# Thirty-two bytes of padding per partition on the split operands of a float32r transformer kernel

## The chip, the cores and the metric

The kernel runs on one core of one Trainium2 chip. The metric is the device time of one execution in microseconds, shown as the median over runs. In the tables below PE is TensorE (matmuls), PEld the loading of its stationary operand, DVE is VectorE, ACT ScalarE, POOL GpSimd and SP SyncE.

## The reference

A sequence of 512 tokens with 1024 features passes through two blocks. The first is a feed-forward layer (SwiGLU), a mixer (dilated-window attention plus a pooled branch, both gated), and a second SwiGLU. The second block has two layers, each a mixer (top-k sparse attention in layer 0, a state-space scan in layer 1) followed by a convolutional feed-forward:

```python
def swiglu(x, w1, w3, w2):
    return (jax.nn.silu(x @ w1) * (x @ w3)) @ w2
...
def conv_ffn(h, w_up, conv_w, conv_b, w_down):
    up = h @ w_up
    up = lax.conv_general_dilated(
        up, conv_w[:, None, :], window_strides=(1,), padding=[(CONV_W - 1, 0)],
        dimension_numbers=('NWC', 'WIO', 'NWC'), feature_group_count=2 * D_FF) + conv_b
    val, gate = jnp.split(up, 2, axis=-1)
    return (jax.nn.silu(gate) * val) @ w_down
```

D_MODEL is 1024, D_FF is 2816, and everything is float32.

## The kernel before

**Three matmuls for one product.** Activations lie feature-major: eight tiles of 128 features by 512 tokens. Each float32 factor is split into a high part h (rounded to float32r by an ACT copy) and a low part l (the rest, by a subtraction), and a product is made of three float32r matmuls (`mm3`, L260 to L262): weight-high times activation-high, weight-high times activation-low, weight-low times activation-high. In `gemm` the stationary operand is 128 columns of a weight tile, and the moving operand is a whole activation tile of 512 columns. In `token_gemm` it is the other way round: 128 tokens of an activation tile are stationary, the weight tile moves. Some of its calls take every fourth token (`by4`), so that the stationary operand is read with a stride of four elements.

**Weights.** `weight` (L238 to L247) issues one DMA of 512 KB into a `raw` tile on SP's queue, copies it to `wh` on ACT (L245) and subtracts it into `wl`, nearly always on DVE (L246). There are four `raw` buffers and three each of `wh` and `wl`.

**Activations.** `xt()` gives tiles of pool `xp` (24 buffers, name `x`). They hold the residual stream and the split inputs of every feed-forward, of the mixer and of the gated unit after the scan. In the feed-forwards the gated product is split into `u` tiles (pool `up`, 16 buffers, opened anew for each feed-forward), which are the moving operands of the second product. The mixer keeps its later split operands in tiles `mu` and `m`, the sparse attention in `du`; the change doesn't touch those.

**Order.** The program runs in this order: SwiGLU 1, mixer, SwiGLU 2, sparse attention, convolutional feed-forward 0, scan and gated unit, convolutional feed-forward 1. The order of instructions on each engine is that of the code; `pump()` slips pieces of background work (modulation vectors, top-k selection, state-space preparation) between weight tiles.

**Where the tiles lie.** Pools are laid one after another in each partition's memory, and the buffers of a pool follow each other without a gap. An `x`, `u` or `t` buffer has 2048 bytes, a `raw`, `wh` or `wl` buffer 4096, all multiples of 512. So all buffers of a pool have one offset modulo 512, and a pool that follows a pool of such buffers has the same one. In the program as built these offsets are:

| tiles | offset modulo 512 bytes |
|---|---|
| raw, wh, wl, x, t | 224 |
| u in both SwiGLUs and in convolutional feed-forward 1 | 224 |
| u in convolutional feed-forward 0 (behind the pool of the state-space preparation) | 96 |
| mu and m (mixer) | 0 |
| du (sparse attention) | 384 |

A 128-column slice of a weight tile starts at a multiple of 512 bytes in it, so the stationary operand of `gemm` is always at 224.

Of the kernel before, what the change touches and what calls it, by code (L numbers as in the profile page):

```python
# [12 lines left out]
F32R = mybir.dt.float32r  # L13
# [6 lines left out]
P = 128  # L20
T = 512
# [151 lines left out]
def emit(nc, tc, A, out):  # L173
    es = ExitStack()
    with es:
        cp = es.enter_context(tc.tile_pool(name="cp", bufs=1))
        raw = es.enter_context(tc.tile_pool(name="raw", bufs=4))
        wp = es.enter_context(tc.tile_pool(name="wp", bufs=3))
        xp = es.enter_context(tc.tile_pool(name="xp", bufs=24))
# [6 lines left out]
        def nm(s):  # L186
            uid[0] += 1
            return f"{s}{uid[0]}"

        def xt(dt=F32):  # L190
            return xp.tile([P, T], dt, name=nm("x"), tag="x")

        def tt(w=T, dt=F32):
            return tp.tile([P, w], dt, name=nm("t"), tag="t")
# [13 lines left out]
        def col(name, k):  # L208
            return vec[:, VEC[name][0] + k : VEC[name][0] + k + 1]
# [13 lines left out]
        def pump():  # L223
            rate[1] += rate[0]
            while rate[1] >= 1.0:
                rate[1] -= 1.0
                while bg:
                    try:
                        next(bg[0])
                        break  # L230
                    except StopIteration:
                        bg.pop(0)
# [6 lines left out]
        def weight(ap, w=1024, eng=V):  # L239
            pump()  # L240
            r = raw.tile([P, 1024], F32, name=nm("raw"), tag="raw")
            nc.sync.dma_start(r[:, :w], ap)
            h = wp.tile([P, 1024], F32R, name=nm("wh"), tag="wh")
            l = wp.tile([P, 1024], F32R, name=nm("wl"), tag="wl")
            S.activation(h[:, :w], r[:, :w], AF.Copy)  # L245
            eng.tensor_tensor(l[:, :w], r[:, :w], h[:, :w].bitcast(F32), op=ALU.subtract)  # L246
            return h, l  # L247

        X = []
        for k in range(KT):  # L250
            t = xt()
            nc.sync.dma_start(t, A["xT"][:, k])
            X.append(t)
            if k == 0:
                first = weight(A["f1u"][0])
# [8 lines left out]
        def gemm(w, XH, XL, o=0, ps=None):  # L264
            ps = psa() if ps is None else ps
            n = len(XH)
            for k in range(n):
                s = slice((o + k) * P, (o + k + 1) * P)
                mm3(ps, w[0][:, s], w[1][:, s], XH[k], XL[k], k == 0, k == n - 1)
            return ps  # L270
# [45 lines left out]
        def spread(y, o=0):  # L316
            p = psb()
            for b in range(4):
                E.matmul(
                    p[:, b * P : (b + 1) * P],  # L320
                    y[:, o + b : o + b + 1].to_broadcast([P, P]), ident, start=True, stop=True,
                )
            return p

        def kept(p):
            t = cp.tile([P, T], F32, name=nm("rb"), tag="rb")
            S.activation(t, p, AF.Copy)
            return t

        def norm(parts):  # L330
            p = psb()
            meansq(p, 0, parts)
            v = const([P, 4])
            V.tensor_scalar(v, p[:, :4], 1e-6, None, op0=ALU.add)
            for j in range(1, len(parts)):
                V.tensor_tensor(v, v, p[:, 8 * j : 8 * j + 4], op=ALU.add)
            y = const([P, 4])
            rsq(v, y, 4)
            return y

        def split_scaled(t, g):
            h, l = xt(F32R), xt(F32R)
            S.activation(h, t, AF.Copy, scale=g)  # L343
            V.scalar_tensor_tensor(l, t, g, h.bitcast(F32), op0=ALU.mult, op1=ALU.subtract)
            return h, l
# [37 lines left out]
        def swiglu_ffn(name, gname, up, acc, then, pre=()):  # L383
            pre = list(pre)
            XH, XL = [], []
            for k in range(KT):
                h, l = split_scaled(X[k], col(gname, k))
                XH.append(h)
                XL.append(l)
            Rb = None  # L390
            for f0, n in FGROUPS:
                UH, UL = [], []
                for f in range(f0, f0 + n):
                    p1 = gemm(pre.pop(0) if pre else weight(A[name + "u"][2 * f]), XH, XL)
                    if Rb is None:
                        Rb = kept(spread(norm(acc.parts())))
                    p3 = gemm(weight(A[name + "u"][2 * f + 1]), XH, XL)
                    a, b = tt(), tt()
                    V.tensor_tensor(a, p1, Rb, op=ALU.mult)
                    S.activation(a, a, AF.Silu)  # L400
                    V.tensor_tensor(b, p3, Rb, op=ALU.mult)  # L401
                    G.tensor_tensor(b, a, b, op=ALU.mult)  # L402
                    h = up.tile([P, T], F32R, name=nm("u"), tag="u")
                    l = up.tile([P, T], F32R, name=nm("u"), tag="u")
                    S.activation(h, b, AF.Copy)
                    G.tensor_tensor(l, b, h.bitcast(F32), op=ALU.subtract)
                    UH.append(h)
                    UL.append(l)
                for m in range(KT):
                    w = weight(A[name + "d"][m, :, f0 * P : (f0 + n) * P], n * P)  # L410
                    p = gemm(w, UH, UL)
                    V.scalar_tensor_tensor(X[m], p, 0.5, X[m], op0=ALU.mult, op1=ALU.add)
                    if f0 == FGROUPS[-1][0]:
                        for t in then:
                            t.add(m)
# [297 lines left out]
        def modulate(Rb, gs):  # L713
            g, sh = gs
            HH, HL, done = [], [], []
            for k in range(KT):
                t = tt()
                h, l = xt(F32R), xt(F32R)
                with tc.issue_after(done[k - 2].ins) if k > 1 else nullcontext():
                    V.scalar_tensor_tensor(t, X[k], g[:, k : k + 1], Rb, op0=ALU.mult, op1=ALU.mult)  # L720
                S.activation(h, t, AF.Identity, bias=sh[:, k : k + 1])
                done.append(
                    V.scalar_tensor_tensor(l, t, sh[:, k : k + 1], h.bitcast(F32), op0=ALU.add, op1=ALU.subtract)
                )
                HH.append(h)
                HL.append(l)
            return HH, HL, done[-1]
# [258 lines left out]
        def conv_ffn(i, up, acc, then=None):  # L986
            Rb = spread(norm(acc.parts()))
            HH, HL, _ = modulate(Rb, GS["f", i])

            def conv(p, j, t):  # L990
                S.activation(t, p, AF.Identity, scale=col(f"cw{i}", 88 + j), bias=col(f"cb{i}", j))
                V.scalar_tensor_tensor(t[:, 1:], p[:, : T - 1], col(f"cw{i}", 44 + j), t[:, 1:], op0=ALU.mult, op1=ALU.add)
                V.scalar_tensor_tensor(t[:, 2:], p[:, : T - 2], col(f"cw{i}", j), t[:, 2:], op0=ALU.mult, op1=ALU.add)

            for f0, n in FGROUPS:
                UH, UL = [], []
                for f in range(f0, f0 + n):
                    p1 = gemm(weight(A[f"u{i}"][2 * f]), HH, HL)
                    a, b = tt(), tt()
                    conv(p1, f, a)  # L1000
                    p3 = gemm(weight(A[f"u{i}"][2 * f + 1]), HH, HL)
                    conv(p3, f + NF, b)
                    S.activation(b, b, AF.Silu)  # L1003
                    G.tensor_tensor(b, a, b, op=ALU.mult)  # L1004
                    h = up.tile([P, T], F32R, name=nm("u"), tag="u")
                    l = up.tile([P, T], F32R, name=nm("u"), tag="u")
                    S.activation(h, b, AF.Copy)  # L1007
                    G.tensor_tensor(l, b, h.bitcast(F32), op=ALU.subtract)  # L1008
                    UH.append(h)
                    UL.append(l)  # L1010
                for m in range(KT):
                    w = weight(A[f"d{i}"][m, :, f0 * P : (f0 + n) * P], n * P)
                    p = gemm(w, UH, UL)
                    V.scalar_tensor_tensor(X[m], p, MOD[i][:, 40 + m : 41 + m], X[m], op0=ALU.mult, op1=ALU.add)  # L1014
                    if f0 == FGROUPS[-1][0]:
                        if then is None:
                            nc.sync.dma_start(out[:, m], X[m])
                        else:
                            then.add(m)
# [327 lines left out]
```

## Time and profile before

| what | value |
|---|---|
| median of 3 runs | 2470.77 us (2466.86 to 2472.44) |
| span of the profiled execution | 2468.1 us |
| PE busy | 2341.6 us, 95% of the span |
| DVE busy | 1479.9 us, 60% |
| ACT busy | 886.5 us, 36% |
| POOL busy | 704.5 us, 29% |
| mean granted TensorE clock | 0.974 of full |

The profile gives the span from the first to the last instruction. For the profiled execution no device time is given beside it; its span is 2.7 us below the median of the runs. Matmuls are pipelined: the duration printed for one (about 0.39 us) is longer than the distance to the next, so the number to read is a stretch's length over its matmuls.

### The profile page before, as it was taken

To read this page: it belongs to the slowest core of one execution; us is meant where nothing else is said; L and a number is where in the kernel's file an instruction comes from. 1 tells how busy PE (TensorE), PEld (TensorE's weight loads), DVE (VectorE), ACT (ScalarE), POOL (GpSimd) and SP (SyncE) were. 2 spreads that over 40 slices of the span, in tenths; PEclk is the share of its full clock that TensorE was granted. 3 is DMA by queue.
4 is the path that set the end of the run, shared out by engine and by line. 5 is a ranking of instruction groups with operands and counts; after the bars stand their busy time and mean duration, and the time that the engine had idled before them with its cause. 6 is when DMAs were issued, how large, how long until landed. Compare 5 with 4: busy or idle time off the path is not lost.

```text
span 2468.1 us, 31107 instructions
## 1 busy us (share of the span) xinstructions
PE 2341.6 (95%) x11608; PEld 1895.3 (77%) x11608; DVE 1479.9 (60%) x2684; ACT 886.5 (36%) x1394; POOL 704.5 (29%) x885
## 2 busy tenths in 40 slices
PE   7999999989999999999899989999898689999999
PEld 6888888877888888887666568787687567788887
DVE  7555565455675555447996648777644964544443
ACT  3222233533333222234435634434333322433332
POOL 2212022141122121137453314645312530111211
PEclk9999999999999999999999999999998899999999
DMA  5544445323444444232121022344425313233322
GB/s 190 158 146 153 154 140 164 109 84 119 153 158 140 147 160 153 89 95 66 45 69 44 26 86 95 102 154 137 145 86 189 124 53 98 77 94 97 100 92 79
DMA packets 94087, 281.94 MB, mean 114 GB/s; under 512 B 9840, under 2 KB 14832, under 8 KB 91888
## 3 DMA queue, kind: packets, MB, share of 16 engines
q1 hardware_dynamic: 89184, 263.30, 33.9%
q10 hardware_dynamic: 4752, 16.65, 1.9%
q8 instruction: 91, 1.49, 0.3%
q14 instruction: 60, 0.49, 0.1%
HBM read 263.14 MB, written 16.78 MB: 113 GB/s over the span
## 4 chain that ended last, share of the span: by engine, by line
PE 76%; DVE 13%; POOL 5%; issue 3%; ACT 2%; DMA 1%; ACTq 0%; SPq 0%; DVEq 0%; POOLq 0%
PE pa L260 23%; PE pa L261 23%; PE pa L262 23%; DVE wl L246 2%; PE pb L941 1%; DVE z L1255 1%; DMA raw<-in_ada 1%; DVE du L857 1%; DVE sm L856 1%; DVE du L810 1%; PE pb L930 1%; PE pa L906 1%; PE pb L314 1%; POOL st L1027 1%; DVE du L809 1%
## 5 line engine op out<-in xcount | busy, mean ns | idle before, releaser
L261 PE MATMUL pa<-x,wh 128*128 128x512 f32 x1736 | 683.2, 394 | 20.2 <-DVE x L1291 15.7
L260 PE MATMUL pa<-x,wh 128*128 128x512 f32 x1736 | 680.5, 395 | 19.7 <-ACT x L343 7.9
L245 ACT ACTIVATE wh<-raw 128x1024 fp32r<-128x1024 f32 (+2 forms) x380 | 391.8, 1034 | 817.2 <-PE pa L261 650.3
L262 PE MATMUL pa<-x,wl 128*128 128x512 f32 x1736 | 680.4, 392 | 3.2 <-DVE wl L246 3.2
L246 DVE TENSOR_TENSOR wl<-raw,wh 128x1024 fp32r<-128x1024 f32 (+2 forms) x364 | 496.7, 1367 | 243.1 <-ACT wh L245 239.3
L261 PEld LDWEIGHTS pa<-x,wh 128*128 128x128 f32 x1736 | 328.6, 189 | 94.4 <-DVE x L1291 17.2
L260 PEld LDWEIGHTS pa<-x,wh 128*128 128x128 f32 x1736 | 328.5, 190 | 93.6 <-ACT x L1290 8.0
L262 PEld LDWEIGHTS pa<-x,wl 128*128 128x128 f32 x1736 | 328.7, 189 | 73.0 <-DVE wl L246 5.2
L260 PE MATMUL pa<-u,wh 128*128 128x512 f32 x704 | 275.8, 395 | 7.9 <-ACT u L1007 7.9
L262 PE MATMUL pa<-u,wl 128*128 128x512 f32 x704 | 273.7, 392 | 3.0 <-DVE wl L246 3.0
L261 PE MATMUL pa<-u,wh 128*128 128x512 f32 x704 | 275.6, 392 | 0.5 <-POOL u L1008 0.5
L368 DVE SCALAR_TENSOR_TENSOR ada<-raw,c,ada 128x512 f32<-128x512 f32 x168 | 130.1, 775 | 220.0 <-DMA raw<-in_ada 218.8
L402 POOL TENSOR_TENSOR t<-t,t 128x512 f32<-128x512 f32 x44 | 72.4, 1646 | 496.6 <-DVE t L401 286.1
L1004 POOL TENSOR_TENSOR t<-t,t 128x512 f32<-128x512 f32 x44 | 57.7, 1311 | 428.5 <-ACT t L1003 422.0
L260 PEld LDWEIGHTS pa<-u,wh 128*128 128x128 f32 x704 | 133.1, 189 | 39.7 <-ACT u L1007 8.8
L260 PE MATMUL pa<-wh,x 128*128 128x512 f32 (+1 forms) x384 | 151.1, 401 | 9.1 <-ACT wh L245 4.5
L262 PEld LDWEIGHTS pa<-u,wl 128*128 128x128 f32 x704 | 132.7, 189 | 32.7 <-DVE wl L246 4.2
L261 PEld LDWEIGHTS pa<-u,wh 128*128 128x128 f32 x704 | 133.0, 189 | 30.1 <-POOL u L1008 1.4
L262 PE MATMUL pa<-wh,x 128*128 128x512 f32 (+1 forms) x384 | 150.9, 396 | 0.0
L261 PE MATMUL pa<-wl,x 128*128 128x512 f32 (+1 forms) x384 | 150.4, 392 | 0.0
L288 POOL TENSOR_TENSOR acc<-acc,t 128x512 f32<-128x512 f32 x45 | 73.5, 1639 | 170.9 <-ACT t L282 160.7
L1014 DVE SCALAR_TENSOR_TENSOR x<-pa,c,x 128x512 f32<-128x512 f32 x48 | 35.5, 748 | 117.9 <-PE pa L262 117.9
(361 smaller groups left out, 3078.7 us busy)
## 6 DMA issues: line engine op xcount, KB each, us to landing
raw<-in_ada SPq DMA_DIRECT2D x96, 512.0 KB, 3.9
raw<-in_u SPq DMA_DIRECT2D x88, 512.0 KB, 3.6
raw<-in_f1u SPq DMA_DIRECT2D x44, 512.0 KB, 4.0
raw<-in_f2u SPq DMA_DIRECT2D x44, 512.0 KB, 3.7
raw<-in_d SPq DMA_DIRECT2D x32, 512.0 KB, 3.6
raw<-in_aq SPq DMA_DIRECT2D x28, 512.0 KB, 3.8
dr<-res SPq DMA_DIRECT2D x8, 1536.0 KB, 7.5
raw<-in_wpg SPq DMA_DIRECT2D x20, 512.0 KB, 3.7
```

Source lines behind the costliest of these rows:

```text
L245: S.activation(h[:, :w], r[:, :w], AF.Copy)
L246: eng.tensor_tensor(l[:, :w], r[:, :w], h[:, :w].bitcast(F32), op=ALU.subtract)
L260: E.matmul(ps, ah, bh, start=first, stop=False)
L261: E.matmul(ps, ah, bl, start=False, stop=False)
L262: E.matmul(ps, al, bh, start=False, stop=last)
L288: G.tensor_tensor(self.sums[0], self.sums[0], sq, op=ALU.add)
L314: E.matmul(p[:, 8 * j + o + b : 8 * j + o + b + 1], a[:, tokens(b, by4)], ones, start=True, stop=True)
L368: V.scalar_tensor_tensor(acc, r[:, j * T : (j + 1) * T], kk, acc, op0=ALU.mult, op1=ALU.add)
L402: G.tensor_tensor(b, a, b, op=ALU.mult)
L809: V.tensor_tensor(dst[:, :, :32], av[:, :, :32], ev[:, :, 32:], op=ALU.subtract)
L1004: G.tensor_tensor(b, a, b, op=ALU.mult)
L1014: V.scalar_tensor_tensor(X[m], p, MOD[i][:, 40 + m : 41 + m], X[m], op0=ALU.mult, op1=ALU.add)
```

## The change

Each `x`, `u`, `wh` and `wl` buffer becomes 32 bytes (eight floats) longer per partition; the code uses the first part of it as before. `raw`, `t` and all other tiles keep their size.

```diff
         def xt(dt=F32):
-            return xp.tile([P, T], dt, name=nm("x"), tag="x")
+            return xp.tile([P, T + 8], dt, name=nm("x"), tag="x")[:, :T]
...
-            h = wp.tile([P, 1024], F32R, name=nm("wh"), tag="wh")
-            l = wp.tile([P, 1024], F32R, name=nm("wl"), tag="wl")
+            h = wp.tile([P, 1024 + 8], F32R, name=nm("wh"), tag="wh")
+            l = wp.tile([P, 1024 + 8], F32R, name=nm("wl"), tag="wl")
...
-                    h = up.tile([P, T], F32R, name=nm("u"), tag="u")
-                    l = up.tile([P, T], F32R, name=nm("u"), tag="u")
+                    h = up.tile([P, T + 8], F32R, name=nm("u"), tag="u")[:, :T]
+                    l = up.tile([P, T + 8], F32R, name=nm("u"), tag="u")[:, :T]
```

The last pair of lines is changed in both feed-forward functions. In the program as built the offsets modulo 512 become: `wh` 224, 256 and 288; `wl` 320, 352 and 384; the 24 `x` buffers and the 16 `u` buffers step by 32 through all sixteen multiples of 32; `raw` stays at 224, `t` goes to 160, `mu` to 448, `du` to 320.

No instruction is added, removed or moved on any engine. One wait is different. On POOL, at the first gated product of convolutional feed-forward 1, the subtraction that makes a `u` tile (L1008, from tile `t`) also waits for a DMA queue and for PE, because its longer pool now overlaps memory of another earlier tile:

```order
 L1004 TENSOR_TENSOR t_16966<-t_16965,t_16966 128x512 [waits Activation_49]
-L1008 TENSOR_TENSOR u_17007<-t_16966,u_17006 128x512 [waits Activation_49]
+L1008 TENSOR_TENSOR u_17007<-t_16966,u_17006 128x512 [waits DMAHW3_49,PE_49,Activation_49]
 L1004 TENSOR_TENSOR t_17042<-t_17041,t_17042 128x512 [waits PE_49,Activation_49]
 L1008 TENSOR_TENSOR u_17083<-t_17042,u_17082 128x512 [waits Activation_49]
```

The row with + has the two more waits, and every row stands where it stood.

## Rows read from the trace of the kernel before

**Rows 1.** The page's head, its engines, and the granted TensorE clock in 40 slices.

```profile
span 2468.1 us, 31107 instructions
PE 2341.6 (95%) x11608; PEld 1895.3 (77%) x11608; DVE 1479.9 (60%) x2684; ACT 886.5 (36%) x1394; POOL 704.5 (29%) x885
PEclk9999999999999999999999999999998899999999
```

**Rows 2.** The page's chain of work that ended last, by engine and by line.

```profile
PE 76%; DVE 13%; POOL 5%; issue 3%; ACT 2%; DMA 1%; ACTq 0%; SPq 0%; DVEq 0%; POOLq 0%
PE pa L260 23%; PE pa L261 23%; PE pa L262 23%; DVE wl L246 2%; PE pb L941 1%; DVE z L1255 1%; DMA raw<-in_ada 1%; DVE du L857 1%; DVE sm L856 1%; DVE du L810 1%; PE pb L930 1%; PE pa L906 1%; PE pb L314 1%; POOL st L1027 1%; DVE du L809 1%
```

**Rows 3.** Waits of ACT, longest first: total us, times, longest.

```profile
ACT wh L245 <- PE pa L261: 650.3, 225, 9.0
```

**Rows 4.** Windows: a stretch (start:end, length), busy time (instructions) by engine, clock.

```profile
107.55:151.07 43.52, 43.52 (x193) 36.04 (x192) 23.08 (x29) 9.68 (x11) 3.42 (x2) 1.00 0.53 168
151.07:238.11 87.04, 87.04 (x385) 72.07 (x384) 49.37 (x56) 26.23 (x31) 21.35 (x14) 1.00 0.46 145
...
2191.58:2235.10 43.52, 43.52 (x193) 36.04 (x192) 16.03 (x17) 10.31 (x12) 2.58 (x2) 1.00 0.32 97
```

**Rows 5.** The same, in the mixer and in convolutional feed-forward 0.

```profile
645.46:656.36 10.90, 10.90 (x49) 9.01 (x48) 6.35 (x7) 3.06 (x4) 1.89 (x1) 1.00 0.53 170
688.01:735.61 47.60, 47.60 (x206) 38.24 (x205) 34.19 (x38) 17.48 (x24) 12.18 (x7) 1.00 0.48 155
...
1604.44:1632.20 27.76, 27.76 (x120) 22.29 (x119) 22.86 (x59) 7.36 (x13) 13.21 (x44) 1.00 0.52 180
1794.71:1860.01 65.30, 65.30 (x290) 54.05 (x288) 30.44 (x35) 25.40 (x34) 12.91 (x10) 1.00 0.28 85
1874.34:1894.17 19.83, 19.83 (x87) 15.95 (x85) 10.56 (x11) 7.40 (x11) 8.14 (x11) 1.00 0.55 157
```

**Rows 6.** PE's timeline in SwiGLU 1 and in convolutional feed-forward 0: start, us, instruction.

```profile
120.47 0.39 PE L260 MATMUL pa<-u,wh 128*128 128x512 f32 x1
120.70 0.39 PE L261 MATMUL pa<-u,wh 128*128 128x512 f32 x1
...
1876.43 0.40 PE L261 MATMUL pa<-u,wh 128*128 128x512 f32 x1
1876.67 0.39 PE L262 MATMUL pa<-u,wl 128*128 128x512 f32 x1
```

**Rows 7.** A window of convolutional feed-forward 0 at half clock.

```profile
1594.30:1598.57 4.27, 4.27 (x10) 3.40 (x11) 0.73 (x2) 0.00 (x0) 4.19 (x6) 0.50 0.00 0
```

**Rows 8.** Windows within `token_gemm`: every fourth token (mixer), neighbouring tokens (sparse attention).

```profile
416.06:436.04 19.98, 19.98 (x86) 19.91 (x86) 8.88 (x10) 8.95 (x16) 5.62 (x13) 1.00 0.34 105
1175.56:1198.05 22.49, 22.49 (x101) 18.58 (x99) 22.28 (x39) 7.77 (x11) 13.38 (x10) 1.00 0.16 48
```

**Rows 9.** The window of the whole span, L260 alone: PE and PEld busy (instructions).

```profile
0.00:2469.00 2469.00, 1166.30 (x2972) 574.78 (x2972) 0.97 0.36 114
```

**Rows 10.** The chain within 0-380, 736-1100, 1100-1466, 1466-1794 and 2100-2480 us.

```profile
by line: PE pa L261 29.6%; PE pa L260 29.5%; PE pa L262 29.4%; issue 3.5%; DMA raw<-in_ada 2.2%; DMA x<-in_xT 1.2%; DVE wl L246 1.1%; DVE x L344 0.9%; DVE ada L368 0.8%; DVE t L280 0.6%; PE pb L314 0.4%; DVE x L412 0.4%; PE pb L319 0.2%; DV
by line: PE pa L261 33.0%; PE pa L260 32.9%; PE pa L262 32.9%; PE pb L314 1.0%; PE pb L319 0.2%; PE pb L377 0.1%
by line: PE pa L260 9.4%; PE pa L261 9.3%; PE pa L262 9.3%; PE pb L941 7.1%; DVE du L857 5.4%; DVE sm L856 4.7%; DVE du L810 4.6%; PE pb L930 4.4%; PE pa L906 3.9%; DVE du L809 3.6%; issue 3.5%; DVE du L851 3.3%; PE pb L906 3.1%; DVE x L723
by line: PE pa L260 11.2%; PE pa L262 10.2%; PE pa L261 10.2%; DVE wl L246 7.7%; issue 6.6%; POOL st L1027 4.1%; POOL res L1032 3.9%; POOL st L1029 3.4%; POOL t L1004 3.3%; POOL res L1031 3.2%; POOL st L1028 3.2%; POOL st L1030 3.1%; POOL u
by line: PE pa L260 32.1%; PE pa L262 31.7%; PE pa L261 31.6%; DVE t L720 0.2%; DVE x L1014 0.2%; ACT x L721 0.2%; PE pb L319 0.1%; issue 0.0%
```

**Rows 11.** Groups in feed-forward 0, then 1: busy us, mean ns, idle before.

```profile
L1008 POOL TENSOR_TENSOR u<-t,u 128x512 fp32r<-128x512 f32 x22 | 29.0, 1316 | 17.3 <-ACT u L1007 17.2
...
L1008 POOL TENSOR_TENSOR u<-t,u 128x512 fp32r<-128x512 f32 x22 | 28.5, 1297 | 36.8 <-ACT u L1007 36.8
```

**Rows 12.** POOL's timeline, the first gated product of convolutional feed-forward 1.

```profile
2129.12 1.39 POOL L1008 TENSOR_TENSOR u<-t,u 128x512 fp32r<-128x512 f32 x1 [0.84 <-ACT u L1007]
```

More of the change, by code (lines that the diff above doesn't have):

```diff
@@ L1004, in conv_ffn @@
                     G.tensor_tensor(b, a, b, op=ALU.mult)
-                    h = up.tile([P, T], F32R, name=nm("u"), tag="u")
-                    l = up.tile([P, T], F32R, name=nm("u"), tag="u")
+                    h = up.tile([P, T + 8], F32R, name=nm("u"), tag="u")[:, :T]
+                    l = up.tile([P, T + 8], F32R, name=nm("u"), tag="u")[:, :T]
                     S.activation(h, b, AF.Copy)
```

## The prediction

> **What bounds the kernel now.** I read the page's head first: PE is busy for 95% of the span and its clock is granted nearly in full [rows 1]. Busy alone is no proof, so the chain of work that ended last comes next: 76% of it is PE, and 69% the three matmuls of the split product, L260 to L262 [rows 2]. Third, the waits: ACT, which rounds the weights, sits 650.3 us in all until PE lets go of a weight buffer [rows 3]. Weights are ready before PE wants them; DMA, ACT and DVE run ahead. The split products hold 89% of the chain in SwiGLU 1 (up to 380 us), 99% in SwiGLU 2 (736 to 1100) and 95% in feed-forward 1 (from 2100), but only 28% in the sparse attention (1100 to 1466) and 32% in feed-forward 0 up to 1794 us [rows 10]. So a change of PE's pace shows in full in most stretches, and in part in these two.
>
> No instruction changes. What can change is how long an instruction takes with its operands elsewhere in memory, so I looked for places in the trace of before where operands already lie at different offsets.
>
> **What the trace says of offsets.** The windows are cut so that they hold nothing but one kind of split product. Their length over their PEld count is the pace of a matmul with its weight load. Where the moving tile and the weight tile are both at 224, the pace is 43.52/192 = 226.67 ns for `u` in SwiGLU 1, 87.04/384 = 226.67 for `x`, and 43.52/192 = 226.67 for `u` in feed-forward 1 [rows 4]. Where they differ it is slower every time: `mu` at 0 against weights at 224 takes 47.60 us for 204 matmuls (the last 12 of a branch product and the 192 of the mixer's final one; the window's 205 counts a neighbour), 233.33 ns; `u` in feed-forward 0, at 96 against 224, takes 27.76/119 = 233.28 and 19.83/85 = 233.29 [rows 5]. The timeline shows the kind of row: same line, same shape, names `u` and `wh`, steps of 0.23 and 0.24 us instead of 0.23 and 0.22 [rows 6].
>
> Could something else in those stages do it? The `x` products beside them answer: in the mixer 10.90/48 = 227.1 ns, between stretches of `mu`, and in feed-forward 0 65.30/288 = 226.74 [rows 5], with the same background work running. Two stretches with POOL busy for 48% and 41% of the time give the same 233.3, as `mu` does with POOL at 26%. So it is the offset, or something that goes with it exactly. The difference is 233.28 - 226.67 = 6.61 ns a matmul.
>
> One condition: at half clock, 1.2 GHz, ten unequal `u` matmuls take 4.27 us, 427 ns each [rows 7]. Twice 213.3; nothing is lost there. The cost belongs to the full clock, 2.4 GHz.
>
> The Trainium skill says otherwise, in "TensorE: Matmul & The Clock Gate", Part 2, step-by-step: PE has two independent read ports, and loading the next tile's weights takes no read bandwidth from the running matmul. By that rule offsets would change nothing and the time would stay; this trace disagrees, 226.67 against 233.28 ns at the same granted clock.
>
> **The change part by part.** There are 2972 matmuls at L260 [rows 9], as many at L261 and L262, 8916 together. Laying the built programs' addresses beside them, 7680 have weights stationary, and 6725 of these run at full clock with equal offsets. Afterwards `x` and `u` step through sixteen offsets and the weights through six, so only 499 of the 6725 stay equal, 46 others become equal, and net 6180 lose it. At 6.61 ns each that is 40.9 us if all of it counts. By stretch:
>
> - SwiGLU 1, mixer, SwiGLU 2, the last third of feed-forward 0, and feed-forward 1, where PE holds the chain (in the mixer I count it so for the gated products and the last one): 1448 + 446 + 1459 + 225 + 1500 = 5078, 33.6 us, taken in full.
> - The gated unit after the scan: 317, of which some 48 are slipped in while the scan has the chain: 269, 1.8 us.
> - The sparse attention's first and last products: 101, 0.7 us.
> - Feed-forward 0 up to 1794 us: 684, 4.5 us; here the chain is PE to a third, with DVE and POOL preparing the state space between. I take half, 2.3 us.
>
> `token_gemm` with neighbouring tokens runs at 22.49/99 = 227.2 ns with equal offsets [rows 8]; unequal, it should go to 233.3, 6.1 ns more. Full-width price for 174 of them in the mixer is 1.1 us, of which I take half (some have half the columns); 614 in the sparse attention would be 3.7 us, and with the chain at 28% I take 1.1. With every fourth token the stationary operand is strided and the pace is 19.98/85 = 235.06 ns already (its 86th count is a neighbour) [rows 8]; I expect no change.
>
> What costs nothing: POOL's subtraction on `u` at 96 and at 224 takes 1316 and 1297 ns and waits for ACT before it [rows 11]: 19 ns on a step that is not late. Were the weight split as much slower, it would lie under ACT's 650 us of waiting [rows 3]; with that cover gone it would cost the same few ns a weight. The wait added on POOL stands at 2129.12 us [rows 12] and is for transfers and matmuls of the scan, the stage before, whose results this feed-forward's first product already used. Behind it only the next gated product is queued, for which PE waits several weights later; the row now stands 0.84 us idle for ACT, and that wait stays the last.
>
> Sum: 33.6 + 1.8 + 0.7 + 2.3 + 0.5 + 1.1 = **40.0 us**. Against its own span, 2468.1 becomes 2508; the median lies 2.7 us above that span and I keep the distance: 2470.8 + 40.0 = **2511 us**, 1.6% slower. With nothing hidden it is 40.9 + 4.8 = 45.7, 2516; with the PE-bound stretches alone 33.6, 2504.
>
> **The unknown in it.** The trace shows three unequal differences (moving minus stationary, modulo 512): 384 and 288 in [rows 5], and 160 in the few `du` products, too short for a window. Afterwards all sixteen occur, about evenly. Of the 6226 that lose equality 1228 land on a difference seen before, 4998 on one of the twelve unseen. Bounds for those, by the nearest rows: as equal ones, 226.67, the change costs 1228 x 6.61 = 8.1 us (2479); as the strided loads, 235.06, 8.1 + 4998 x 8.39 = 50.0 us (2521); as if nothing were lost, half of the 427 ns, 213.5, a gain of 65.8 - 8.1 = 57.7 us (2413). I take 233.3, since the two that could be measured agree to 0.1 ns though far apart.
>
> **The rivals.**
>
> 1. *Only some differences cost* (small ones, say, behave as equal). With half of the twelve free, 24.6 us: 2495. For it: the nearest seen to zero is 128 away. Against: no grading among those seen. Chance 0.11.
> 2. *Unseen differences are worse*, as the strided loads: 2521, or 2526 with nothing hidden. For it: the strided row shows that PE can be held longer. Against: no unstrided stretch above 233.4. Chance 0.07.
> 3. *No change, 2471.* The slow stretches are slow for a reason that goes with their stage and not with the offset, and PE reads both operands without loss wherever they lie. For it: all slow stretches have background work beside them. Against: so have the `x` stretches next to them, at 227 [rows 5]. Chance 0.05. The Trainium skill's rule of the two read ports, cited above, is this case.
> 4. *Faster.* Equal offsets are not free either: 226.67 is 13.2 ns over half of 427. If the unseen differences avoided that loss, the time would fall to 2413; it decides from an average below 226.67 - 8.1/4.998 = 225.05 ns over them. Against: all three unequal differences went the other way. Chance 0.05.
>
> The forecast, 2504 to 2516 by its own bounds, has 0.72.
>
> **How the numbers follow.** A difference below 0.2% (5 us) can hardly be told from none here: the three runs span 5.6 us. Forecast and rivals 1 and 2 are slower by more: 0.90; same 0.05; faster 0.05. The range leaves out rivals 3 and 4 and the lower half of rival 1 (0.05): from 2490 to 2524, where half-free differences (2495) and strided pace (2521) fall inside, and the uncertainty of what is hidden besides.
>
> **What would show it.** Right: in feed-forward 1 the `u` stretches of 192 matmuls go from 43.5 to about 44.7 us, the `x` stretches of 384 from 87.0 to about 89.4 (one in fourteen stays equal); `u` in feed-forward 0 keeps 233; PE's busy time rises by about 40 us and the durations of ACT, DVE and POOL stay. ACT's wait for PE grows. Wrong: `u` and `x` stretches still at 226.67 (rival 3), a spread by buffer with some at 226.67 and some at 233 (rival 1), above 235 (rival 2), or below 225 (rival 4). A mean near 233 without the time rising would mean that I took the cover of the chain wrongly.

## The result, and the profile after

The changed kernel is slower: its executions take 2492.6, 2495.06 and 2497.01 us, against 2466.86 to 2472.44 (median 2470.1, four executions) before. The ratio is 1.0104, 95% interval 1.0088 to 1.012. (A fourth execution of the changed kernel lasted 11045 us at full granted clock; it is left out of every comparison.) The span of the profiled one grew from 2468.1 to 2493.3 us, by 25.2. The forecast was 2511 us with a range of 2490 to 2524: the direction and the kind of work were right, the size was 40 us where 25 came.

The head of the page of the changed kernel, its engines, and the chain by engine:

```profile
span 2493.3 us, 31108 instructions
PE 2373.6 (95%) x11608; PEld 1896.1 (76%) x11608; DVE 1480.0 (59%) x2684; ACT 887.4 (36%) x1394; POOL 709.4 (28%) x885
...
PE 75%; DVE 13%; POOL 5%; issue 3%; ACT 2%; DMA 2%; ACTq 0%; SPq 0%; DVEq 0%; POOLq 0%
```

Compared with [rows 1, 2], PE is busy 32.0 us longer with the same 11608 matmuls; ACT and DVE are as they were (+0.9 and +0.1 us), POOL has 4.9 us more, 3.9 of it in the scan's stage. ACT's wait for PE, its largest, grew from 650.3 us [rows 3] by 45; weights are ready still earlier than PE wants them:

```profile
ACT wh L245 <- PE pa L261: 695.1, 231, 9.2
```

The windows of the changed kernel over stretches of one kind of split product (start:end, length, busy us and count of PE, PEld, DVE, ACT, POOL, then clock). In order: `u` and `x` in SwiGLU 1, `mu` in the mixer, `u` in convolutional feed-forward 0, `u` and `x` in 1:

```profile
109.26:153.75 44.49, 44.49 (x193) 36.05 (x192) 22.78 (x28) 9.61 (x11) 3.43 (x2) 1.00 0.49 166
153.75:242.67 88.92, 88.92 (x385) 72.11 (x384) 50.33 (x56) 26.25 (x31) 21.76 (x14) 1.00 0.44 142
696.16:743.49 47.33, 47.33 (x206) 38.30 (x204) 32.16 (x37) 17.52 (x24) 10.59 (x7) 1.00 0.44 146
1620.71:1648.29 27.58, 27.58 (x120) 22.29 (x119) 22.30 (x61) 7.36 (x13) 13.46 (x44) 1.00 0.54 182
2210.58:2255.13 44.55, 44.55 (x193) 36.06 (x192) 16.11 (x17) 10.31 (x12) 2.58 (x2) 1.00 0.29 95
2255.13:2344.16 89.03, 89.03 (x385) 72.20 (x384) 41.50 (x47) 35.05 (x46) 18.15 (x14) 1.00 0.30 95
```

Length over PEld count is the pace again: 231.7, 231.6, 232.0, 231.8, 232.0 and 231.8 ns. The stretches that ran at 226.67 [rows 4] lost about 5 ns a matmul, and the two that already ran at 233.3 [rows 5] *won* 1.3 and 1.5 ns, where `u` in feed-forward 0 was to keep its 233. All now have one pace, below the 233.3 that I had put in for every unequal offset.

The stages of the program, first before and then after, cut at the same PE instruction. In order: SwiGLU 1, mixer, SwiGLU 2, sparse attention, feed-forward 0 up to its last third, that last third, scan and gated unit, feed-forward 1. Before:

```profile
7.90:380.10 372.20, 367.72 (x1610) 302.02 (x1611) 225.65 (x263) 110.74 (x135) 85.41 (x55) 1.00 0.49 156
380.10:736.10 356.00, 343.70 (x1707) 288.74 (x1706) 205.96 (x352) 132.03 (x229) 80.45 (x111) 0.98 0.41 129
736.10:1100.10 364.00, 364.00 (x1635) 301.79 (x1633) 188.54 (x217) 109.95 (x133) 83.59 (x55) 1.00 0.43 134
1100.10:1466.10 366.00, 335.58 (x1660) 242.24 (x1660) 263.19 (x691) 168.56 (x394) 157.39 (x155) 0.95 0.17 53
1466.10:1794.00 327.90, 305.13 (x1385) 246.84 (x1384) 246.40 (x719) 134.29 (x205) 153.97 (x382) 0.96 0.38 126
1794.00:1900.00 106.00, 103.48 (x462) 84.67 (x461) 49.77 (x66) 39.94 (x53) 23.65 (x23) 1.00 0.35 106
1900.00:2080.00 180.00, 142.75 (x1496) 115.82 (x1495) 122.76 (x165) 54.44 (x75) 62.31 (x51) 0.90 0.34 115
2080.00:2464.00 384.00, 378.80 (x1664) 313.16 (x1663) 175.07 (x211) 133.52 (x168) 56.94 (x44) 0.98 0.29 90
```

After:

```profile
8.03:387.44 379.41, 374.95 (x1610) 302.12 (x1610) 226.51 (x263) 110.83 (x135) 85.86 (x55) 1.00 0.47 153
387.44:743.95 356.51, 345.32 (x1706) 288.52 (x1705) 205.29 (x350) 132.07 (x229) 79.49 (x111) 0.98 0.39 127
743.95:1115.57 371.62, 371.62 (x1634) 301.89 (x1633) 191.23 (x218) 110.42 (x133) 84.03 (x56) 1.00 0.41 132
1115.57:1481.83 366.26, 336.74 (x1660) 241.38 (x1660) 264.46 (x691) 168.44 (x394) 157.55 (x155) 0.96 0.17 53
1481.83:1809.07 327.24, 307.22 (x1385) 246.86 (x1384) 245.10 (x719) 134.54 (x205) 154.73 (x382) 0.96 0.38 126
1809.07:1916.19 107.12, 104.58 (x462) 84.64 (x461) 49.74 (x66) 39.95 (x53) 23.67 (x23) 1.00 0.33 104
1916.19:2097.99 181.80, 146.85 (x1496) 118.14 (x1495) 119.97 (x165) 54.46 (x75) 66.22 (x51) 0.88 0.33 114
2097.99:2489.15 391.16, 385.97 (x1665) 312.52 (x1663) 175.16 (x211) 133.63 (x168) 57.09 (x44) 0.99 0.28 88
```

Read the first number behind each window (the length) and the second (PE busy). In the two SwiGLUs and feed-forward 1 both grew alike, by 7.2, 7.6 and 7.2 us. In the sparse attention PE is busy 1.2 us longer and the stage 0.3; in the first two thirds of feed-forward 0 PE has 2.1 us more and the stage is 0.7 *shorter*; in the mixer 1.6 and 0.5. The lengths add up to 25.0 us, PE's busy time to 32.1: 7 us of PE's added busy time filled time in which PE waited anyway (2.3 of them in the scan and gated unit, where the clock also fell from 0.90 to 0.88). So two questions stay: why 5 ns and not 6.61, and is it the offset at all?

### The profile page after: what moved, and what is told of

It is laid out like the page before. It is cut to its first block, busy times and chain, and to the rows that moved or that the text cites. A ratio compares the mean times of both kernels' runs of the same rounds, so it can differ in the third digit from the quotient of the medians.

```text
span 2493.3 us, 31108 instructions
## 1 busy us (share of the span) xinstructions
PE 2373.6 (95%) x11608; PEld 1896.1 (76%) x11608; DVE 1480.0 (59%) x2684; ACT 887.4 (36%) x1394; POOL 709.4 (28%) x885
## 4 chain that ended last, share of the span: by engine, by line
PE 75%; DVE 13%; POOL 5%; issue 3%; ACT 2%; DMA 2%; ACTq 0%; SPq 0%; DVEq 0%; POOLq 0%
PE pa L260 23%; PE pa L262 23%; PE pa L261 23%; DVE wl L246 2%; DVE z L1255 1%; DMA raw<-in_ada 1%; PE pb L941 1%; DVE du L857 1%; DVE sm L856 1%; DVE du L810 1%; PE pa L906 1%; ACT wh L245 1%; PE pb L930 1%; DVE du L809 1%; POOL res L1032 1%
## 5 line engine op out<-in xcount | busy, mean ns | idle before, releaser
L261 PE MATMUL pa<-x,wh 128*128 128x512 f32 x1736 | 690.5, 398 | 17.0 <-DVE x L1291 12.5
L260 PE MATMUL pa<-x,wh 128*128 128x512 f32 x1736 | 688.4, 399 | 17.5 <-ACT x L343 8.0
L262 PE MATMUL pa<-x,wl 128*128 128x512 f32 x1736 | 688.3, 397 | 4.5 <-DVE wl L246 4.5
L260 PEld LDWEIGHTS pa<-x,wh 128*128 128x128 f32 x1736 | 328.9, 190 | 99.1 <-ACT x L343 8.0
L260 PE MATMUL pa<-u,wh 128*128 128x512 f32 x704 | 277.9, 398 | 8.0 <-ACT u L1007 7.9
L1004 POOL TENSOR_TENSOR t<-t,t 128x512 f32<-128x512 f32 x44 | 57.9, 1316 | 433.1 <-ACT t L1003 433.1
L260 PEld LDWEIGHTS pa<-u,wh 128*128 128x128 f32 x704 | 133.0, 189 | 42.1 <-ACT u L1007 8.8
L260 PE MATMUL pa<-wh,x 128*128 128x512 f32 (+1 forms) x384 | 152.3, 404 | 7.7 <-ACT t L874 3.5
```

The lines of the kernel that those rows point to most:

```text
L260: E.matmul(ps, ah, bh, start=first, stop=False)
L261: E.matmul(ps, ah, bl, start=False, stop=False)
L262: E.matmul(ps, al, bh, start=False, stop=last)
```

## The experiments

Two theories, called A and B. **A:** each difference between the moving and the stationary offset has its own price, some lower than 6.61 ns, and a stretch with many differences pays the mean of their prices. **B:** every unequal difference costs the same 6.6 ns once PE has settled into it, and the changed kernel, whose difference changes from matmul to matmul, is faster than 233.3 because it never settles. The rival to both is that the cost comes from something else: the longer buffers themselves, the place in memory rather than the difference, or the background work.

The first two runs do one half of the change each, the next two hold the difference constant, and the other four test what those left over. The kernel before was timed beside each four: median 2467.54 us (7 executions), then 2467.12 (15).

### Weights alone, activations alone

```diff
+            h = wp.tile([P, 1024 + 8], F32R, name=nm("wh"), tag="wh")
+            l = wp.tile([P, 1024 + 8], F32R, name=nm("wl"), tag="wl")
```

> Only wh and wl buffers are 32 bytes longer; x and u stay at offset 224. Theory A (each pair of moving and stationary offsets has its own price, and a flat one for any unequal pair): 2 of 9 matmuls stay equal, so 0.78 x 6725 x 6.6 ns = 34 us of PE time, some 2500 us. Theory B (a stretch with one constant difference settles into 226.7 ns if equal or 233.3 ns if not; a stretch whose offsets change from matmul to matmul settles into neither and runs at about 231.7 as in the changed kernel): the weight offset changes within every three matmuls, so about 231.7 ns, +25 us, near 2496. Theory C (the changed activation offsets alone matter): no change, 2470.

```diff
+            return xp.tile([P, T + 8], dt, name=nm("x"), tag="x")[:, :T]
...
+                    h = up.tile([P, T + 8], F32R, name=nm("u"), tag="u")[:, :T]
+                    l = up.tile([P, T + 8], F32R, name=nm("u"), tag="u")[:, :T]
```

> Only x and u buffers are 32 bytes longer; all weights stay at 224. One in sixteen moving tiles is equal. Theory A with a flat price: 0.94 x 6725 x 6.6 ns = 42 us of PE time, some 2505 us, pace 232.9. Theory B: the offset changes with every matmul, pace about 231.7, +25 us, near 2496. Theory C': if the weights' own change of offset were what costs, no change, 2470.

Measured: 2501.29 us, ratio 1.0132 (1.0112 to 1.0151), and 2506.86 us, ratio 1.0146 (1.0128 to 1.0165). The window of 384 `x` matmuls in SwiGLU 1, weights alone:

```profile
157.56:246.69 89.13, 89.13 (x385) 72.09 (x384) 50.89 (x56) 26.27 (x31) 20.64 (x14) 1.00 0.45 142
```

Activations alone, the same window (its 385 counts a neighbour), and the stage of the sparse attention:

```profile
157.73:246.91 89.18, 89.18 (x386) 72.33 (x385) 49.59 (x56) 26.25 (x31) 22.69 (x14) 1.00 0.45 142
1121.80:1493.99 372.19, 345.34 (x1661) 246.77 (x1660) 264.71 (x692) 168.73 (x394) 157.46 (x155) 0.93 0.17 52
```

That is 232.1 and 232.2 ns: either half alone makes nearly the pace of the whole change, though the weights' half has six weight offsets and no longer activation buffer, and the other has untouched weights. The halves don't add up, as two costs of longer buffers would. What is unequal matters, not which side got longer.

One point of the first expectation was wrong. The six longer weight buffers also push the pools behind them by 192 bytes, so in the program as built `x` stands at 416 and not at 224, and no `x` product has equal offsets: the differences are 192, 160 and 128 to `wh`, and 96, 64 and 32 to `wl`.

Neither half is cheaper than the whole; that activations alone come out slower than the whole is mostly not the pace. 5.9 us of it is in the sparse attention (372.19 us against 366.26), where the granted clock of that execution is 0.93 and not 0.96. The first stage, too, is 11.8 us longer than before in both halves and 7.2 in the changed kernel; it differs by some 4 us between executions without any change of pace, as with all offsets equal (below), where it is 3.8 us longer than before. The difference lies at its start: steps of 427 ns, as at half clock [rows 7], go on up to 21 us in the kernel before and up to 30 us there (the profile's record of the clock starts only behind them). The window from 20 to 32 us, before and with all offsets equal, holds 58 and 40 matmuls:

```profile
20.00:32.00 12.00, 12.00 (x58) 9.82 (x57) 10.81 (x20) 1.06 (x1) 1.51 (x1) 1.00 0.42 129
20.00:32.00 12.00, 12.00 (x40) 9.80 (x39) 10.15 (x17) 1.06 (x1) 1.54 (x1) 1.00 0.38 117
```

The two theories are not told apart yet: B has an unsettled pace for both halves, and A has 232.8 ns for the weights alone by the prices found below, 0.7 above the measured 232.1.

### Constant differences

A pool with one small tile ahead of another moves everything behind it, and no buffer gets longer. `leads` are the bytes ahead of the `u` pool of each of the four feed-forwards.

```diff
+        gap = es.enter_context(tc.tile_pool(name="gx", bufs=1))
+        gap.tile([P, 8], F32, name="gx", tag="gx")
...
+        leads = iter((32, 96, 352, 448))
```

> No buffer is longer; gaps ahead of pools give every stretch one constant difference (moving minus stationary, modulo 512): x 32, u 64 in SwiGLU 1, 128 in SwiGLU 2, 256 in feed-forward 0, 480 in feed-forward 1, mu 320. Theory A in the form of a table by difference: paces that differ from stretch to stretch, lying around 231.7, some of them below 231. Theory B: 233.3 in every one of them, and a time of about 2511, longer than with the changed kernel although each tile is laid without padding. Rival of the prediction that near differences behave as equal: x at 32 and u at 480 run at 226.7.

Measured: 2498.45 us, one execution. Its windows, in order: `u` at a difference of 64 (192 matmuls), `x` at 32 (384), `mu` at 320 (204), `u` at 128 (192), `u` at 256 (113; PEld counts a neighbour here and at `mu`), `u` at 480 (192):

```profile
110.16:154.11 43.95, 43.95 (x194) 36.06 (x192) 21.44 (x26) 9.17 (x10) 3.67 (x2) 1.00 0.51 164
154.11:243.70 89.59, 89.59 (x385) 71.96 (x384) 48.16 (x56) 26.27 (x31) 23.74 (x14) 1.00 0.45 143
697.35:744.05 46.70, 46.70 (x206) 38.31 (x205) 33.45 (x38) 17.51 (x24) 12.08 (x7) 1.00 0.49 156
835.42:880.03 44.61, 44.61 (x193) 36.17 (x192) 23.60 (x30) 9.15 (x10) 3.42 (x2) 1.00 0.52 163
1623.71:1649.33 25.62, 25.62 (x115) 21.17 (x114) 21.53 (x52) 6.09 (x9) 13.26 (x44) 1.00 0.55 186
2212.24:2257.04 44.80, 44.80 (x193) 36.06 (x192) 16.10 (x17) 10.31 (x12) 2.60 (x2) 1.00 0.29 94
```

The paces are 228.9, 233.3, 228.9, 232.3, 226.7 and 233.3 ns. **B falls here**: four of the six are constant and unequal and don't stand at 233.3. And 256 bytes apart costs nothing. SwiGLU 2 checks the prices against the end time: 1056 `x` matmuls at +6.65 and 528 `u` at +5.7 are 7.0 + 3.0 = 10.0 us, and its stage is 374.0 us, 10.0 more than before.

```diff
+        gap.tile([P, 64], F32, name="gx", tag="gx")
...
+        leads = iter((352, 96, 320, 160))
```

> As the run before with other constants: x 256, u 96 in SwiGLU 1, 352 in SwiGLU 2, 448 in feed-forward 0, 416 in feed-forward 1, mu 32. Theory A as a table: other paces around 231.7; with a modulus of 256 instead of 512, x runs at 226.7. Theory B: 233.3 throughout, some 2511 us.

Measured: 2481.53 us, one execution. `u` at 96, `x` at 256, `u` at 352, `u` at 448 in feed-forward 0 (113 matmuls), `u` at 416:

```profile
111.37:156.19 44.82, 44.82 (x194) 36.04 (x192) 22.42 (x28) 9.30 (x11) 3.42 (x2) 1.00 0.53 164
156.19:243.27 87.08, 87.08 (x386) 72.09 (x384) 49.32 (x56) 26.22 (x31) 21.32 (x14) 1.00 0.46 145
829.75:874.56 44.81, 44.81 (x193) 36.04 (x192) 24.47 (x31) 9.16 (x10) 3.42 (x2) 1.00 0.50 159
1614.58:1640.94 26.36, 26.36 (x114) 21.19 (x113) 21.74 (x57) 6.09 (x9) 13.38 (x44) 1.00 0.55 190
2199.30:2244.28 44.98, 44.98 (x193) 36.16 (x192) 16.11 (x17) 10.31 (x12) 2.57 (x2) 1.00 0.32 94
```

233.4, 226.8, 233.4, 233.3 and 234.3 ns: 256 again costs nothing, now over 384 matmuls, and 96 and 352, which are 256 apart, agree, as 64 and 320 did.

### Place or difference

Here the gap stands ahead of the weights, so that weights and activations move together by 160 bytes and `x` stays equal to them, at 384 instead of 224.

```diff
+        gap = es.enter_context(tc.tile_pool(name="gw", bufs=1))
+        gap.tile([P, 40], F32, name="gw", tag="gw")
...
+        leads = iter((160, 192, 0, 224))
```

> Gaps again, no longer buffers: weights and x together move to offset 384 (difference 0), u gets the constant differences 160 in SwiGLU 1, 192 in SwiGLU 2, 384 in feed-forward 0 and 224 in feed-forward 1. If the difference alone decides and its modulus is 256: x 226.7 as at 224; 160 as 416 (234.2), 192 as 448 (233.3), 224 as 480 (233.3). If 224 itself was a favoured place, x loses and runs at 233.

Measured: 2482.5 us, one execution. `u` at a difference of 160, `x` at 0, `u` at 192, `u` in feed-forward 0 at 384 (119 matmuls), `u` in feed-forward 1 at 224:

```profile
111.21:156.19 44.98, 44.98 (x193) 36.16 (x192) 22.62 (x27) 9.15 (x10) 2.78 (x2) 1.00 0.52 164
156.19:243.24 87.05, 87.05 (x385) 72.10 (x384) 50.64 (x56) 26.24 (x31) 20.64 (x14) 1.00 0.46 145
829.47:874.27 44.80, 44.80 (x193) 35.91 (x192) 24.12 (x30) 9.15 (x10) 3.43 (x2) 1.00 0.50 160
1615.26:1642.91 27.65, 27.65 (x120) 22.37 (x119) 22.38 (x59) 7.33 (x13) 13.23 (x44) 1.00 0.53 181
2200.68:2245.48 44.80, 44.80 (x193) 36.07 (x192) 16.11 (x17) 10.32 (x12) 2.58 (x2) 1.00 0.29 94
```

`x` runs at 226.7 ns at its new place: the difference decides, not the place. `u` gives 234.3, 233.3, 232.4 and 233.3. At the difference 384 the kernel before had 233.28 [rows 5], 0.9 ns more. The place doesn't make this either: a third stretch of that same kernel, with every buffer where it was in the other two (95 `u` matmuls of feed-forward 0), ran at 232.5:

```profile
1772.62:1794.71 22.09, 22.09 (x97) 17.90 (x95) 8.02 (x12) 3.22 (x4) 0.00 (x0) 1.00 0.49 166
```

So this difference has two paces, and what chooses between them stays open.

### Equal offsets everywhere

The reverse of the change. No split buffer gets longer; gaps bring `u` of feed-forward 0, `mu`, `m` and `du` to 224 as well.

```diff
+        leads = iter((0, 0, 128, 0))
...
+                mt([P, 56])
...
+                small(dg, [P, 88])
```

> No buffer is longer; gaps of 128, 224 and 352 bytes ahead of u in feed-forward 0, of the mixer's tiles and of the attention's du bring the moving operands that were unequal in the kernel before to 224, like their weights. If the offset is the cause, those stretches go from 233.3 to 226.7 ns: 528 u, about 350 mu and m, 96 du, 6.4 us of PE time at most, of which 3 should show: 2467 against 2470. If the slow pace belongs to those stages' background work, they stay at 233 and the time at 2470.

Measured: 2463.81 us (11 executions), ratio to before 0.998, 95% interval 0.9969 to 0.999: faster than both kernels, by 3.3 us than the one before, where some 3 were expected. `mu`, 204 matmuls, and `u` in feed-forward 0, 119:

```profile
689.27:735.51 46.24, 46.24 (x205) 38.30 (x204) 33.38 (x38) 17.54 (x24) 12.14 (x7) 1.00 0.50 160
1602.76:1629.75 26.99, 26.99 (x120) 22.29 (x119) 22.40 (x59) 7.34 (x13) 13.20 (x44) 1.00 0.52 184
```

226.7 and 226.8 ns, where [rows 5] had 233.3 with the same background work: POOL is busy 13.20 of 26.99 us in the second. So the slow stretches of before were slow for their offsets, and not for the background work of their stage. Half of the 6.4 us of PE time that was at stake showed in the time.

### Longer buffers with a harmless step

`u` buffers get 512 bytes longer in SwiGLU 1, 256 in SwiGLU 2, none in feed-forward 0 and 128 in feed-forward 1.

```diff
+                    h = up.tile([P, T + grow[0]], F32R, name=nm("u"), tag="u")[:, :T]
+                    l = up.tile([P, T + grow[0]], F32R, name=nm("u"), tag="u")[:, :T]
```

> x and the weights as before; u buffers longer by 512 bytes in SwiGLU 1, 256 in SwiGLU 2, none in feed-forward 0, 128 in feed-forward 1. With modulus 256 the first two cost nothing although buffers are longer and, in the second, lie at two offsets modulo 512: 226.7 both; with modulus 512 the second would run between 226.7 and 233. The third kind alternates between differences 0 and 128 (modulo 256): by the table of single differences (226.7 and 232.4 or 233.3) a mean of 229.5 to 230; if a sequence that changes never settles, about 231.7.

Measured: 2468.89 us, one execution. `u` with a step of 512, of 256, of 128 (192 matmuls each), and the last 84 matmuls with 128:

```profile
107.53:151.05 43.52, 43.52 (x194) 36.04 (x193) 23.23 (x29) 9.69 (x11) 3.44 (x2) 1.00 0.52 165
824.38:867.90 43.52, 43.52 (x194) 36.04 (x192) 24.28 (x31) 9.16 (x10) 3.43 (x2) 1.00 0.48 158
2188.87:2232.92 44.05, 44.05 (x193) 36.01 (x192) 16.10 (x17) 10.31 (x12) 2.59 (x2) 1.00 0.30 96
2443.43:2462.97 19.54, 19.54 (x85) 15.78 (x84) 6.93 (x9) 1.70 (x2) 0.00 (x0) 1.00 0.29 98
```

226.67 and 226.67 ns: longer buffers cost nothing where the step keeps the difference at 0 modulo 256. With a step of 128, in the program as built, the high parts of `u` stand 0 or 256 from the weights in both of these stretches, and the low parts 128 or 384. A product reads the high part in two of its three matmuls, so one in three is unequal, and the mean by price is (2 x 226.7 + 232.4) / 3 = 228.6 ns. The first stretch gives 229.4, near it. The last gives 232.6 with the same pattern of differences, which no mean of those two prices reaches. Taken apart by the starts in the trace, the steps after the first, second and third matmul of a product are 227.9, 233.2 and 227.1 ns in the first stretch and 234.6, 232.6 and 230.5 in the last. A mixture isn't just the mean, and the same mixture can have two paces.

### One load in three

`wl` gets a pool of its own, 128 bytes behind `wh` modulo 512, with gaps that keep `x` and `u` equal to `wh`. Two of every three products stay equal.

```diff
+        g1.tile([P, 32], F32, name="g1", tag="g1")
+        wq = es.enter_context(tc.tile_pool(name="wq", bufs=3))
...
+        g2.tile([P, 96], F32, name="g2", tag="g2")
...
-            l = wp.tile([P, 1024], F32R, name=nm("wl"), tag="wl")
+            l = wq.tile([P, 1024], F32R, name=nm("wl"), tag="wl")
```

> Only the wl buffers move, to 128 bytes behind wh modulo 512; x and u stay equal to wh. One matmul in three is then unequal (difference 384, settled price 233.3). By the table of single differences: (2 x 226.7 + 233.3) / 3 = 228.9 ns, and some 15 us more. If a change within three matmuls keeps the pace from settling: nearer 231.7, 25 to 30 us more.

Measured: 2495.74 us, one execution, 28.6 us above the kernel before. The window of 384 `x` matmuls:

```profile
157.31:246.05 88.74, 88.74 (x385) 72.64 (x384) 48.50 (x56) 26.23 (x31) 23.55 (x14) 1.00 0.45 143
```

and from the groups by line of a stretch of feed-forward 1, where the three matmuls of `mm3` are L265 to L267 in this kernel (busy us, mean ns of one, idle before):

```profile
L267 PE MATMUL pa<-x,wl 128*128 128x512 f32 x106 | 42.1, 397 | 0.0
L266 PE MATMUL pa<-x,wh 128*128 128x512 f32 x106 | 42.0, 396 | 0.0
L265 PE MATMUL pa<-x,wh 128*128 128x512 f32 x107 | 41.6, 389 | 0.0
```

231.1 ns, where the mean of two equal matmuls and one unequal would be (2 x 226.67 + 233.3) / 3 = 228.9. Taken apart by the starts in the trace, the step after the first matmul of a product (the next load is `wh`) is some 227 ns, after the second (the next load is `wl`, 128 bytes off) 232.4 to 232.6, and after the third (the next is `wh` again) 234.0 to 234.3. The groups show the same: two of the three matmuls are 7 and 8 ns longer, although only one has unequal weights. One odd load costs two steps here.

## Why the prediction was right, and where it was off

**Right: what bounds the kernel and what the change does to it.** PE's pace moved, ACT and DVE didn't, and the time followed in the stages where PE holds the chain. The difference between moving and stationary offset is the cause: it was shown by moving both sides (226.7 ns at a new place), by moving each alone (232.1 and 232.2), by longer buffers without a difference (226.67) and by taking the difference away (233.3 to 226.7 and 226.8). Rival 3, no change, falls with it, and so does rival 4: no difference ran below 226.7. The same instruction with the same loads runs at 226.67 or at up to 234.3 ns, at a granted clock of 1.00 in all these windows. By the Trainium skill's rule of the two read ports ("TensorE: Matmul & The Clock Gate", Part 2, step-by-step) loading the next weights takes no read bandwidth from the running matmul. The traces disagree in so far as the weights' place changes the pace; whether it is read bandwidth that is lost, no run shows.

The condition held as well. At half clock, by the starts in the traces, 48 steps with equal offsets take 426.6 ns (all offsets equal), and 46 with offsets 32 bytes apart 426.7 (first run with constant differences).

**Off: the price.** The step that failed is "I take 233.3" for the twelve unseen differences, from two that could be measured. That they agreed to 0.1 ns was chance, as 384 also runs at 232.4, and two of sixteen say little of the others:

| difference modulo 512 | ns a matmul, constant difference |
|---|---|
| 0, 256 | 226.7, 226.8 |
| 64, 320 | 228.9, 228.9 |
| 128, 384 | 232.3, 232.4 (233.3 and 232.5 in the kernel before) |
| 32, 192, 224, 288, 448, 480 | 233.3 each |
| 96, 352 | 233.4, 233.4 |
| 160, 416 | 234.3, 234.3 |

What counts is the difference modulo 256. Rival 1, "only some differences cost", was right in kind, but not in its guess that the small ones are free: 32 pays in full. That its time, 2495 us, is the measured one is luck: it had half of the twelve unseen differences free, while only 256 is, and 64 and 320 cost a third of the price. The forecast's range holds the result because its lower end was put below that rival. Over the sixteen the mean is 231.95 ns, and the changed kernel ran at 231.6 to 232.0. The net 6180 matmuls at 6.61 ns were to cost 40.9 us; at the measured 231.7, 5.0 ns on all 6725 that had been equal is 33.8, beside PE's +32.0 us of busy time. The counts pair each matmul with the load that follows it; in the program as built 7764 matmuls have weights stationary, not 7680, and paired with its own load a matmul stays equal in 381 cases, not 499, which moves the 40.9 us by less than 1. Rival 2 has its one case, 160 and 416, 1 ns above most others.

The table's mean is close, yet the changed kernel doesn't consist of settled prices: laid out by the next load's difference, its steps run from some 230 to 233 ns, and the 540 or so equal ones stand at 230.5, not at 226.7. The last experiment shows why that can be: a step next to an unequal one pays too. So A has the prices, but its mean is met here in part by luck: it misses by 0.7 ns with the weights alone (232.8 for 232.1), by 2.2 with one odd load in three (228.9 for 231.1) and by 4.0 in the last stretch with a step of 128 (228.6 for 232.6). B was wrong on the level and had a part of the truth on the mixture.

**Off: the cover.** Four PE-bound stretches, SwiGLU 1 and 2, feed-forward 1 and the last third of feed-forward 0, were to give 4632 x 6.61 = 30.6 us and gave 23.1, by the price. The other terms: the scan's gated unit 1.8 and measured 1.8, which is luck, since PE's busy time there grew by 4.1 us at a lower clock; but the mixer 2.9 + 0.5, the sparse attention 0.7 + 1.1 and the rest of feed-forward 0 2.3, together 7.5 us, measured 0.5, 0.3 and -0.7, together 0.1. The mixer's was taken in full and the others by half or by the chain's share. PE was busy 1.6, 1.2 and 2.1 us longer there, and little of that reached the stage's end. In three other runs (weights alone, the first with constant differences, one load in three) PE was busy 4.4 to 6.0 us longer in these three stages, and together they came out 1.0 to 2.3 us shorter than before. At 5.0 instead of 6.61 ns the sum of 40.0 would have been some 30.5; so of the 15 us between 40.0 and 25.0 about 9.5 are the price and 5.5 the cover. A stage varies by up to 4 us between executions, so the sign of the small ones is not to be read.

**Steps that cost nothing, as forecast.** The subtraction that makes `u` on POOL takes 1321 and 1304 ns, with 1316 and 1297 in [rows 11]. The added wait, on POOL's timeline of the changed kernel:

```profile
2146.39 1.41 POOL L1008 TENSOR_TENSOR u<-t,u 128x512 fp32r<-128x512 f32 x1 [0.83 <-ACT u L1007]
```

Before it POOL is idle 0.83 us, for ACT, as it was 0.84 us in [rows 12].

**`token_gemm`.** Neighbouring tokens go from 227.2 [rows 8] to 231.6 ns, where 233.3 was forecast; every fourth token from 235.06 to 236.2, where no change was. Both are small beside the rest.

**What stays open.** Why the period is 256 bytes, and by what mechanism the two places matter to each other, no run here shows. Why 384 and the step of 128 have two paces each, and why even equal offsets stay 13.2 ns above half of the half-clock step of [rows 7], neither.

## What to carry to other kernels

Where PE is the bound at full clock and each matmul comes with a load of its weights, look at the addresses of both operands: the same start modulo 256 bytes gave the best pace here, and padding that staggered the buffers took it away. Buffer lengths that are multiples of 256 keep it by themselves; a pool behind an odd-sized one may need a gap; such gaps won 0.2% here. When a price is taken from the few cases that a trace happens to show, the cases not seen deserve a range of their own, and so does the share that shows in stages where the bounding engine waits: of 4.9 us of added PE time there 0.1 showed here, and of the 6.4 that equal offsets were to save, half.

## What the runs showed of the hardware

Not expected: the pace of a 128x128 by 512 float32r matmul depends on the distance of its operands modulo 256 bytes, 226.7 to 234.3 ns, in a pattern that isn't ordered by size (64 costs 2.2 ns, 32 costs 6.6). A single unequal load among two equal ones slowed two steps, to some 232.5 and 234.1 ns instead of 226.7. One sequence of differences ran at two paces in one execution, 229.4 and 232.6 ns. And where one execution was granted a clock of 0.93 instead of 0.96 in the sparse attention, that stage was 5.9 us longer than in the changed kernel.
